# ScalarE's inputs of a state-space scan queued earlier, and two Toeplitz tables filled while it runs

## The chip, the cores and the metric

The kernel runs on one core of a Trainium2 chip. The metric is the device time of one execution in microseconds. A core has TensorE (matrix products, with a queue for weight loads), VectorE, ScalarE and GpSimd, and SyncE, which only issues transfers. Each engine takes its instructions in the order in which the program issues them, and engines wait for one another through semaphores.

## The reference

Two encoder layers of 512 tokens and 1024 channels. The change touches the mixer of the first: a projection to three parts, a gated depthwise convolution of 31 taps with a layer norm (`ya`), a bidirectional diagonal complex scan over 32 groups of 16 channels with 64 states (`yb`), and an output product. Feed-forward, neighbourhood attention and a second feed-forward follow.

```python
z = h @ w_in                                  # 1024 -> 512 za, 512 zg, 512 u
a = za * sigmoid(zg)
a = conv1d_depthwise(a, conv_w, taps=31) + conv_b
ya = silu(layer_norm(a, ln_g, ln_b))
# scan, for each direction: x_t = A x_{t-1} + coef * (B u_t); y_t = Re(C x_t)
dt = exp(log_step); mag = exp(lr * dt)
ar = mag * cos(li * dt); ai = mag * sin(li * dt)
y = y_fwd + y_bwd + d_skip * u
y = gelu(y)
yb = y * sigmoid(y @ glu_w + glu_b)
h = concatenate([ya, yb]) @ w_out
```

## The kernel before

All tokens stay on the chip. Weights stream from memory in chunks of 512 KB; `Weights` (lines 50 to 114) holds three raw buffers. The first 12 chunks (`ab_w_in`) are used as they land. Every later one is split by `split()` into `whi`, a rounded copy by ScalarE (line 89), and `wlo`, the rest by VectorE (line 91); then the next load is issued on SyncE's queue. `ahead()` splits two chunks beyond the current one, or, while `hold` is set, only loads.

The schedule is written by hand: what the program issues first on an engine runs first on it. Only VectorE's filling work is metered: `bgV.tick(ns)` adds a credit and issues steps of waiting generators as long as it is positive, and `charge` takes credit away. A step of 512 columns costs 75 + 512/0.96 = 608.

Stages in order, with the lines of the profile:

- Parameters and `u`: x is transposed and `u = xg @ W` is formed in four chunks (line 638). Between them VectorE makes the powers, phases and the first tables `PB` (`make_pb`). ScalarE writes `CT`, evicts `u` into `un` (line 677); `to_chunks` transposes that into `U`.
- The scan runs in eight pieces of four groups. `piece_t(i)` transposes `PB[i]` to `ppb` (evicted by ScalarE, 799) and copies two halves of C into `CB[i % 2]` (803); `piece_k(i)` multiplies `PB` by `CB` to kernel taps `kf` (813, 816); `piece_v(i)` multiplies `ppb` by `U` to `vt` (827, 830). `g_turn(i)` makes a phase table on VectorE, whose negated copy is ScalarE's (763). `g_scan(i)` is VectorE's work: ScalarE writes the decays `dk` in tile `rstdB` (770), then come a product with the phase, the scan instruction (781), a second product and sums into `S2`.
- In iteration i the order is `piece_v(i)`, three projection steps, T and K of piece i+2, four projection steps, `g_scan(i)`, `g_turn(i+2)`, `make_pb(i+4)`. A projection step (`heavy`, 694) is a matmul of zg or za, 64 in all; the last eight follow the loop, with VectorE's products `an` (703).
- Behind it `kd` is written to memory. The convolution (952) is a product of `AC`, the transposed `an`, with Toeplitz tables: 16 pieces n, two to a slot, three slots. `make_tc` fills a slot by 16 ScalarE instructions (925), each with a column of `mask16` as its factor; the first slot is filled by VectorE (930). Beside it VectorE makes the output tables `Q` (48 metered steps) and gathers each four pieces (960, 962).
- T (the banded kernel) is loaded from `kd` in three transfers (967, 969) issued behind the convolution. `out_y` needs T, `U`, `S2` and `Q`; the first is followed by the layer norm's mean (1026), its variance (1039), transposes (1052), the gelu, and the products `wo` and `glu`, which take split weights.

The lines around the change's largest move:

```python
piece_v(i); heavy(HV[0])
if i + 2 < NPC: pieces_tk(i + 2)      # P, ppb, CB, K, kf
heavy(HV[1]); run(g_scan(i))          # begins with ScalarE's decays
if i + 2 < NPC: run(g_turn(i + 2))    # ends with ScalarE's sign copy
if i + 4 < NPC: make_pb(i + 4)
```

Of the kernel before, what the change touches and what calls it, by code (L numbers as in the profile page):

```python
# [9 lines left out]
F32 = mybir.dt.float32  # L10
F32R = mybir.dt.float32r
I32 = mybir.dt.int32
AF = mybir.ActivationFunctionType
# [12 lines left out]
KW, VW = 64, 64  # L26
# [88 lines left out]
def tile_hybrid_encoder(ctx, tc, x, mix_norm, ffn_norm, ffn_w_gate, ffn_w_up, ffn_w_down,  # L115
# [60 lines left out]
    def psb(name="psb"):  # L176
        return psp.tile([P, 512], F32, tag="b", name=name, bufs=4)
# [154 lines left out]
    def pt(shape, name, pool=None, dt=F32):  # L332
        return (pool or mp).tile(shape, dt, tag=name, name=name)
# [19 lines left out]

    vecs = pt([NROW, P], "vecs", ep)
    work = pt([P, 2, 512], "work", ep)
    un = pt([P, G, 4, 16], "un", ep)
    lam = pt([96, 2, 64], "lam", ep)
    lst = pt([96, 2], "lst", ep)
    cwn = ep.tile([TAPS, 4, P], F32, tag="vt", name="cwn", bufs=2)
# [258 lines left out]
    for k in range(KD):  # L618
# [2 lines left out]
        A.activation(out=t, in_=pxs[k], func=AF.Copy)  # L621
        xT.append(t)


    pu = [psa("u") for _ in range(4)]
    for i in range(4):
# [7 lines left out]
        for kk in range(2):  # L634
            k = 2 * i + kk
            for j in range(4):
                c = slice(j * P, (j + 1) * P)
                PE.matmul(out=pu[j], lhsT=xg[:, k, c], rhs=w[:, kk], start=(k == 0), stop=(k == 7))
        if i == 1:
            rs0 = rsqrt(ss, 4, 1e-6, 1.0 / D)  # L640
            hrs = tmp([P, 4], "hrs", 1)
            V.tensor_scalar(out=hrs, in0=rs0, scalar1=0.5, scalar2=None, op0=ALU.mult)
# [22 lines left out]
        if i == 2:  # L665
            for r in range(2):
                ps = psb("ct")
                for t in range(4):
                    PE.transpose(out=ps[:, t * P:(t + 1) * P],
                                 in_=cnat[r][:, t].rearrange("p d n -> p (d n)"), identity=ident)  # L670
                A.activation(out=CT[:, r], in_=ps.rearrange("p (g c) -> p g c", c=16), func=AF.Copy,
                             scale=-1.0 if r else 1.0)
            for v, q, r, sg in ((0, 0, 0, 1.0), (0, 1, 1, 1.0), (1, 0, 1, -1.0), (1, 1, 0, 1.0)):
                A.activation(out=low[v][:, :, :, q], in_=et[:, r, :, 0].rearrange("p e g -> p g e"), func=AF.Copy,
                             scale=sg)
    for j in range(4):
        A.activation(out=un[:, :, j], in_=pu[j].rearrange("p (g c) -> p g c", c=16),
                     func=AF.Copy, scale=rs0[:, j:j + 1])


    an = pt([P, G, 4, 16], "an")
# [26 lines left out]
    def g_proj():  # L708
        yield from proj(True)
        yield from proj(False)  # L710

    proj_all = g_proj()

    def heavy(n):
        for _ in range(n):
# [33 lines left out]
    def g_turn(i):  # L749

        e = phases[i % 2]
        phase[i] = e
        sh = [P, 4, 8, 16]
        gs = slice(4 * i, 4 * i + 4)
        w = [pbt(sh) for _ in range(2)]
        for r in range(2):
            high = et[:, r, :, 1, gs].rearrange("p e g -> p g e").unsqueeze(3).to_broadcast(sh)
            lo = low[r][:, gs].rearrange("p g b q -> p g (b q)").unsqueeze(2).to_broadcast(sh)
            yield tt(w[r], high, lo, ALU.mult)
        yield tt(e[:, 1:3].rearrange("p q (n b) -> p n b q", b=8),  # L760
                 w[0].rearrange("p g a (b q) -> p (g a) b q", q=2),
                 w[1].rearrange("p g a (b q) -> p (g a) b q", q=2), ALU.add)
        A.activation(out=e[:, 0], in_=e[:, 2], func=AF.Copy, scale=-1.0)

    def g_scan(i):

        gs = slice(4 * i, 4 * i + 4)
        e = phase.pop(i)
        v, dk = vin.pop(i), decays[:, i % 2]
        A.activation(out=dk[:, :, 1:], in_=m8[:, 1, gs].unsqueeze(2).to_broadcast([P, 4, NCH - 1]), func=AF.Copy)  # L770
        m = work.rearrange("p o (q n) -> p o q n", q=2)
        z = tmp([P, 2, 256], "sqacc")

# [12 lines left out]
        yield tt(S2[0:64, :, gs, 1:NCH], mv[0:64, :, 0], mv[0:64, :, 1], ALU.add)  # L786
        yield tt(S2[64:128, :, gs, NCH - 2::-1], mv[64:128, :, 0], mv[64:128, :, 1], ALU.add)

    kd = dr.tile([8, 16, 1024], F32, name="kd")
    kf = pt([P, 2, G, 16], "kf", ep)  # L790
    ppb = xp.tile([P, 4, 2, 4, P], F32, tag="xgl", name="ppb")

    def piece_t(i):
        for q in range(2):
            ps = psb("P")
            for g in range(4):
                PE.transpose(out=ps[:, g * P:(g + 1) * P],
                             in_=PB[i][:, q, g].rearrange("p b c -> p (b c)"), identity=ident)
            A.activation(out=ppb[:, i % 4, q], in_=ps.rearrange("p (g n) -> p g n", g=4), func=AF.Copy)
        cb = CB[i % 2]  # L800
        for d in range(2):
            h = slice(64 * d, 64 * d + 64)
            A.activation(out=cb[h, :, :, d], in_=CT[h, :, 4 * i:4 * i + 4], func=AF.Copy)

    def piece_k(i):
        g0 = 4 * i
        pb, cb = PB.pop(i), CB[i % 2]
        pk = psb("K")
        for g in range(4):
            for q in range(2):  # L810
                w = pb[:, q, g].rearrange("p b c -> p (b c)")
                for c in range(0, P, KW):
                    PE.matmul(out=pk[c:c + KW, g * 32:g * 32 + 32], lhsT=w[:, c:c + KW],
                              rhs=cb[:, q, g].rearrange("p d c -> p (d c)"),
                              start=(q == 0), stop=(q == 1))
        A.activation(out=kf[:, :, g0:g0 + 4],
                     in_=pk[:, 0:128].rearrange("p (g d c) -> p d g c", g=4, d=2), func=AF.Copy)

    def piece_v(i):

        g0 = 4 * i
        pp = ppb[:, i % 4]
        pv = psb("v")
        for q in range(2):
            for g in range(4):
                for c in range(0, P, VW):
                    PE.matmul(out=pv[c:c + VW, (q * 4 + g) * 64:(q * 4 + g + 1) * 64], lhsT=pp[:, q, g, c:c + VW],
                              rhs=U[:, g0 + g] if c == 0 else U[:, g0 + g, ::-1], start=True, stop=True)
        v = ep.tile([P, 2, 256], F32, tag="vt", name="vt", bufs=2)
        A.activation(out=v, in_=pv.rearrange("p (q n) -> p q n", q=2), func=AF.Copy)  # L830
        vin[i] = v

    def pieces_tk(*ii):
        for i in ii:
            piece_t(i)
            piece_k(i)

    pieces_tk(0, 1)
    to_chunks(un, U)
    run(g_turn(0))  # L840
    make_pb(3)
    run(g_turn(1))
    for i in range(NPC):
        piece_v(i)
        heavy(HV[0])
        if i + 2 < NPC:
            pieces_tk(i + 2)
        heavy(HV[1])
        run(g_scan(i))
        if i + 2 < NPC:  # L850
            run(g_turn(i + 2))
        if i + 4 < NPC:
            make_pb(i + 4)
        if i == 1:
            V.tensor_tensor(out=gqk, in0=col[:, R_QK:R_QK + 1], in1=col[:, R_QK + 1:R_QK + 2], op=ALU.mult)
    for h in range(2):
        PL.tensor_tensor(out=pair[:, 64 * h:64 * h + 64], in0=ident[:, 0:64], in1=ident[:, 64:128], op=ALU.add)
    PL.tensor_scalar(out=pair, in0=pair, scalar1=1.0 / 512, scalar2=1.0, op0=ALU.mult, op1=ALU.mult)
# [20 lines left out]
    nc.sync.dma_start(out=kd_ap(9, 3), in_=kfr[16:64, 1])  # L879
    PL.dma_start(out=kd_ap(7, 1), in_=kfr[0:16, 1], accum_op=ALU.add)  # L880

    V.tensor_reduce(out=mask16, in_=ident.rearrange("p (b c) -> p c b", c=16), axis=AX.X, op=ALU.add)
    heavy(100)
    W.hold = False
    early.close()
# [21 lines left out]
    for h in range(2):  # L907
        src = conv_b[0, 256 * h:256 * h + 256]
        nc.sync.dma_start(out=cbB[64 * h:64 * h + 64],
                          in_=bass.AP(tensor=src.tensor, offset=src.offset, ap=[[0, 64], [1, 256]]))  # L910
    tca = lp.tile([P, 2, 2, 2, 16, NLAG], F32, name="tca", tag="tca")
    slots = [tca[:, 0], tca[:, 1]]
    wvs = wv.rearrange("p (h s) l -> p h s l", h=2)
    tcs = {}

    def make_tc(n, cnt=2):

        t = slots[n // 2 % 3]
        for i in range(cnt):
            tcs[n + i] = t[:, :, (n + i) % 2]  # L920
        t = t[:, :, n % 2:n % 2 + cnt]
        w = wvs[:, :, n:n + cnt]
        if n > 1:
            for c in range(16):
                A.activation(out=t[:, :, :, c], in_=w, func=AF.Copy, scale=mask16[:, c:c + 1])
            return
        sh = [P, 16, NLAG]
        for h in range(2):
            for i in range(cnt):
                V.tensor_tensor(out=t[:, h, i], in0=w[:, h, i].unsqueeze(1).to_broadcast(sh),  # L930
                                in1=mask16.unsqueeze(2).to_broadcast(sh), op=ALU.mult)
        bgV.charge(1700 * cnt)

    job_q = {(i, hf): g_q(i, hf) for i, hf in ((0, 0), (2, 0), (0, 1), (2, 1), (1, 0), (3, 0), (1, 1), (3, 1))}
    bgV.fill += job_q.values()
    make_tc(0, 1)
    make_tc(1, 1)
    slots.append(xp.tile([P, 2, 2, 16, NLAG], F32, tag="xgh", name="tcb"))
    tick(1000)
    to_chunks(an, AC[:, :, 2:NCH + 2])  # L940
    make_tc(2)
    make_tc(4)
    yc = pt([P, LCH, 16, 16], "an")
    lns = tmp([P, 4, LCH], "lns", 1)
    for b in range(4):
        ps = psa("conv")
        for gi in range(4):
# [8 lines left out]
            if n % 2 and n + 5 < 16:  # L956
                make_tc(n + 5)
            tick(2200)
        gs = slice(4 * b, 4 * b + 4)
        V.tensor_tensor(out=yc[:, :, gs], in0=ps.rearrange("p (g c t) -> p t g c", g=4, t=LCH),  # L960
                        in1=cbB[:, gs].unsqueeze(1).to_broadcast([P, LCH, 4, 16]), op=ALU.add)
# [548 lines left out]
```

## Time and profile before

| | us |
|---|---|
| median of 3 runs | 1277.01 (1276.51 to 1278.05) |
| profiled execution | 1276.18 |
| its span | 1274.5 |
| TensorE busy | 1218.3 (96%) |
| VectorE busy | 676.6 (53%) |
| ScalarE busy | 466.6 (37%) |

The span is what the profiler covers; the execution is a little longer. Busy time is an average over stages: a matmul's end is modelled, and an engine that waits for another counts as idle. In what follows, a wait is put down to the instruction that came last, and the timeline's start times count from the start of the span.

### The profile page before, as it was taken

Reading aid. Unit: us, or ns where it says so; the run is one execution under the profiler, and the core shown is the slowest. Engines: PE = TensorE matmul, PEld = TensorE weight load, DVE = VectorE, ACT = ScalarE, POOL = GpSimd, SP = SyncE. Lnnn points to the kernel's source line nnn. Section 1 sums busy time; section 2 is a strip of 40 time slices with the busy share of each in tenths; the row PEclk is TensorE's granted clock in tenths of the full one; section 3 lists DMA queues with packets and bytes.
Section 4 is the critical chain, followed back from the end, with each engine's and each line's share of the span. In section 5 each row is a group of like instructions: output and inputs, shape, how many; then the busy total and the mean of one; then the engine's idle time right before and its main releaser. Section 6 shows DMA issues by size and latency. Waiting matters only on the chain.

```text
span 1274.5 us, 16175 instructions
## 1 busy us (share of the span) xinstructions
PE 1218.3 (96%) x6427; PEld 962.4 (76%) x6427; DVE 676.6 (53%) x1165; ACT 466.6 (37%) x823; POOL 36.7 (3%) x90
## 2 busy tenths in 40 slices
PE   7887967899999999999999999999999999999998
PEld 4544467688888888888888887667888888888886
DVE  7897896665444444333335753655544444443322
ACT  4523296543323322222225455553432233222110
POOL 1000000000000000000000001430000000000000
PEclk9988999899999999999999999999999999999999
DMA  7411230333333333333344353212233333332321
GB/s 154 89 34 34 68 86 2 100 99 88 95 99 97 93 93 99 94 102 93 91 136 157 116 165 104 72 51 66 84 104 95 99 99 100 99 99 86 128 100 33
DMA packets 173154, 118.04 MB, mean 93 GB/s; under 512 B 21193, under 2 KB 153593, under 8 KB 173080
## 3 DMA queue, kind: packets, MB, share of 16 engines
q1 hardware_dynamic: 172616, 115.92, 31.4%
q10 hardware_dynamic: 400, 1.07, 0.4%
q8 instruction: 50, 0.82, 0.3%
q14 instruction: 24, 0.20, 0.0%
q0 software_dynamic: 64, 0.03, 0.0%
HBM read 109.04 MB, written 7.96 MB: 92 GB/s over the span
## 4 chain that ended last, share of the span: by engine, by line
PE 89%; ACT 5%; DVE 3%; DMA 1%; SPq 1%; issue 1%; POOL 0%; DVEq 0%; ACTq 0%; POOLq 0%
PE up L199 6%; PE gate L199 6%; PE gate L200 6%; PE up L200 6%; PE gate L201 6%; PE up L201 6%; PE qkv L1375 3%; PE qkv L1377 3%; PE qkv L1376 3%; PE dn L199 3%; PE dn L201 3%; PE dn L200 3%; PE dn L1476 3%; PE dn L1474 3%; PE dn L1475 3%; PE o L1337 3%
## 5 line engine op out<-in xcount | busy, mean ns | idle before, releaser
L91 DVE TENSOR_TENSOR wlo<-wraw,whi 128x1024 fp32r<-128x1024 f32 x176 | 212.9, 1213 | 262.6 <-ACT whi L89 261.3
L89 ACT ACTIVATE whi<-wraw 128x1024 fp32r<-128x1024 f32 x176 | 183.5, 1045 | 288.9 <-issue 113.9
L199 PE MATMUL gate<-xgh,whi 128*128 128x512 f32 x352 | 137.2, 390 | 0.0
L199 PE MATMUL up<-xgh,whi 128*128 128x512 f32 x352 | 137.1, 390 | 0.0
L201 PE MATMUL gate<-xgh,wlo 128*128 128x512 f32 x352 | 137.0, 389 | 0.0
L201 PE MATMUL up<-xgh,wlo 128*128 128x512 f32 x352 | 137.0, 389 | 0.0
L200 PE MATMUL gate<-xgl,whi 128*128 128x512 f32 x352 | 136.9, 389 | 0.0
L200 PE MATMUL up<-xgl,whi 128*128 128x512 f32 x352 | 136.9, 389 | 0.0
L1159 DVE TENSOR_TENSOR fu<-up,rstdB 128x512 f32<-128x512 f32 x44 | 30.4, 691 | 113.3 <-PE up L201 113.3
L1161 ACT ACTIVATE gh<-fu 128x512 fp32r<-128x512 f32 x44 | 27.8, 632 | 150.8 <-DVE fu L1160 150.8
L201 PEld LDWEIGHTS gate<-xgh,wlo 128*128 128x128 f32 x352 | 66.1, 188 | 14.0
L199 PEld LDWEIGHTS gate<-xgh,whi 128*128 128x128 f32 x352 | 66.1, 188 | 13.7
L201 PEld LDWEIGHTS up<-xgh,wlo 128*128 128x128 f32 x352 | 66.1, 188 | 13.8
L199 PEld LDWEIGHTS up<-xgh,whi 128*128 128x128 f32 x352 | 66.0, 188 | 13.8
L200 PEld LDWEIGHTS up<-xgl,whi 128*128 128x128 f32 x352 | 66.2, 188 | 13.6
L200 PEld LDWEIGHTS gate<-xgl,whi 128*128 128x128 f32 x352 | 66.0, 187 | 13.4
L199 PE MATMUL dn<-gh,whi 128*128 128x512 f32 x176 | 69.3, 394 | 0.0
L200 PE MATMUL dn<-gl,whi 128*128 128x512 f32 x176 | 69.3, 394 | 0.0
L201 PE MATMUL dn<-gh,wlo 128*128 128x512 f32 x176 | 69.3, 394 | 0.0
L1476 PE MATMUL dn<-whi,gl 128*128 128x512 f32 x176 | 69.2, 393 | 0.0
L1474 PE MATMUL dn<-whi,gh 128*128 128x512 f32 x176 | 69.0, 392 | 0.0
L1375 PE MATMUL qkv<-whi,xgh 128*128 128x512 f32 x176 | 68.8, 391 | 0.0
(293 smaller groups left out, 2053.6 us busy)
## 6 DMA issues: line engine op xcount, KB each, us to landing
wraw<-in_ffn_w_gate_dram SPq DMA_DIRECT2D x44, 512.0 KB
wraw<-in_ffn_w_up_dram SPq DMA_DIRECT2D x44, 512.0 KB
wraw<-in_ffn_w_down_dram SPq DMA_DIRECT2D x38, 512.0 KB
wraw<-in_na_w_qkv_dram SPq DMA_DIRECT2D x24, 512.0 KB
wraw<-in_ab_w_in_dram SPq DMA_DIRECT2D x12, 512.0 KB
bt<-bd SPq DMA_DIRECT2D x8, 640.0 KB
wraw<-in_ab_w_out_dram SPq DMA_DIRECT2D x8, 512.0 KB
wraw<-in_na_w_out_dram SPq DMA_DIRECT2D x8, 512.0 KB
```

What stands on the lines that cost most here:

```text
L89: self.nc.scalar.activation(out=hi, in_=raw, func=AF.Copy)
L91: eng.tensor_tensor(out=lo, in0=raw, in1=hi.bitcast(F32), op=ALU.subtract)
L199: PE.matmul(out=o, lhsT=lh, rhs=rh, start=start, stop=False)
L200: PE.matmul(out=o, lhsT=lh, rhs=rl, start=False, stop=False)
L201: PE.matmul(out=o, lhsT=ll, rhs=rh, start=False, stop=stop)
L1337: PE.matmul(out=o[64 * e:64 * e + 64, j * P:(j + 1) * P], lhsT=vt[p0:p0 + n, kt, hc:hc + 64], rhs=pt_[p0:p0 + n, b, e], start=(b == 0), st ...
L1375: PE.matmul(out=pq[j], lhsT=lh, rhs=wh[:, kk], start=(k == 0), stop=False)
L1376: PE.matmul(out=pq[j], lhsT=lh, rhs=wl[:, kk], start=False, stop=False)
L1377: PE.matmul(out=pq[j], lhsT=ll, rhs=wh[:, kk], start=False, stop=(k == 7))
L1474: PE.matmul(out=pd[j], lhsT=gh[:, k, c], rhs=wh[:, kk], start=(k == 0), stop=False)
L1475: PE.matmul(out=pd[j], lhsT=gh[:, k, c], rhs=wl[:, kk], start=False, stop=False)
L1476: PE.matmul(out=pd[j], lhsT=gl[:, k, c], rhs=wh[:, kk], start=False, stop=(k == NF - 1))
```

## The change

`un` moves into the tile that also holds `ppb`, which has two slots instead of four. Of the four evictions of `u`, two go to VectorE. `piece_t` no longer copies C; `make_cb` does, two pieces ahead, and piece 0's P and K are issued between chunks of `u`. The sign copy and the decays become `scan_tables(i)`, issued an iteration ahead of their scan. The two-slot tile `tca` is allocated beside the scan's buffers, `mask16` is formed in iteration 1, and from iteration 2 on six table instructions follow each iteration (`tc_early`, slots for n = 0 to 3); VectorE's fill goes. In the convolution, `W.ahead()` is called behind the second group.

```diff
-    un = pt([P, G, 4, 16], "un", ep)
+    half_xgl = xp.tile([P, 2, 2048], F32, tag="xgl", name="un_ppb")
+    un = half_xgl[:, 0].rearrange("p (g j c) -> p g j c", g=G, j=4)
+    ppb = half_xgl[:, 1].rearrange("p (s q g n) -> p s q g n", s=2, q=2, g=4)
...
+    def make_cb(i):
+        cb = CB[i % 2]
+        for d in range(2):
+            h = slice(64 * d, 64 * d + 64)
+            A.activation(out=cb[h, :, :, d], in_=CT[h, :, 4 * i:4 * i + 4], func=AF.Copy)
...
+            if k == 6:
+                piece_k(0)
...
+            make_cb(0)
+            make_cb(1)
+            piece_t(0)
...
     for j in range(4):
-        A.activation(out=un[:, :, j], in_=pu[j].rearrange("p (g c) -> p g c", c=16),
-                     func=AF.Copy, scale=rs0[:, j:j + 1])
+        v = pu[j].rearrange("p (g c) -> p g c", c=16)
+        if j % 2:
+            V.tensor_scalar(out=un[:, :, j], in0=v, scalar1=rs0[:, j:j + 1], scalar2=None, op0=ALU.mult)
+        else:
+            A.activation(out=un[:, :, j], in_=v, func=AF.Copy, scale=rs0[:, j:j + 1])
...
+    tca = pt([P, 2, 2, 2, 16, NLAG], "tca")
+    def g_tc(n):
+        t = slots[n // 2 % 3]
+        for i in range(2):
+            tcs[n + i] = t[:, :, i]
+        for c in range(16):
+            A.activation(out=t[:, :, :, c], in_=wvs[:, :, n:n + 2], func=AF.Copy, scale=mask16[:, c:c + 1])
+            yield 1
+    def g_tc_early():
+        yield from g_tc(0)
+        yield from g_tc(2)
...
+    def scan_tables(i):
+        e = phase[i]
         A.activation(out=e[:, 0], in_=e[:, 2], func=AF.Copy, scale=-1.0)
+        A.activation(out=decays[:, i % 2, :, 1:], in_=m8[:, 1, 4 * i:4 * i + 4].unsqueeze(2).to_broadcast([P, 4, NCH - 1]),
+                     func=AF.Copy)
...
-        A.activation(out=dk[:, :, 1:], in_=m8[:, 1, gs].unsqueeze(2).to_broadcast([P, 4, NCH - 1]), func=AF.Copy)
...
-    pieces_tk(0, 1)
+    piece_t(1)
     to_chunks(un, U)
+    piece_k(1)
+    make_cb(2)
+    make_cb(3)
     run(g_turn(0))
     make_pb(3)
     run(g_turn(1))
+    scan_tables(0)
+    tc_early = g_tc_early()
     for i in range(NPC):
         piece_v(i)
         heavy(HV[0])
         if i + 2 < NPC:
-            pieces_tk(i + 2)
+            piece_t(i + 2)
+            piece_k(i + 2)
+        if i + 4 < NPC:
+            make_cb(i + 4)
         heavy(HV[1])
+        if i + 1 < NPC:
+            scan_tables(i + 1)
         run(g_scan(i))
...
         if i == 1:
+            V.tensor_reduce(out=mask16, in_=ident.rearrange("p (b c) -> p c b", c=16), axis=AX.X, op=ALU.add)
+        if i > 1:
+            for _ in range(6):
+                next(tc_early, 0)
...
-    V.tensor_reduce(out=mask16, in_=ident.rearrange("p (b c) -> p c b", c=16), axis=AX.X, op=ALU.add)
...
-    make_tc(0, 1)
-    make_tc(1, 1)
+    for _ in tc_early:
+        pass
...
     to_chunks(an, AC[:, :, 2:NCH + 2])
-    make_tc(2)
     make_tc(4)
...
             if n % 2 and n + 5 < 16:
                 make_tc(n + 5)
             tick(2200)
+        if b == 1:
+            W.ahead()
         gs = slice(4 * b, 4 * b + 4)
```

## Rows read from the trace of the kernel before

**Rows 1.** The page: busy tenths of 40 slices; costliest groups (busy, mean ns | idle).
```profile
PE   7887967899999999999999999999999999999998
...
L91 DVE TENSOR_TENSOR wlo<-wraw,whi 128x1024 fp32r<-128x1024 f32 x176 | 212.9, 1213 | 262.6 <-ACT whi L89 261.3
```

**Rows 2.** Waits, 20 to 240 us: who waited <- for whom: total us, times, longest.
```profile
ACT phase L763 <- DVE phase L436: 42.5, 6, 8.4
...
DVE sqacc L781 <- ACT rstdB L770: 12.1, 4, 4.1
...
DVE work L436 <- ACT vt L830: 3.9, 3, 1.9
```

**Rows 3.** Timeline of VectorE (start, duration us, instruction, [idle <-releaser]), the scan's ends.
```profile
48.02 0.69 DVE L436 TENSOR_TENSOR pb<-work 128x512 f32<-128x512 f32 x1
...
59.70 1.22 DVE L436 TENSOR_TENSOR work<-phase,vt 128x1024 f32<-128x1024 f32 x1 [1.94 <-ACT vt L830]
...
153.75 0.37 DVE L882 TENSOR_REDUCE mask<-ident 128x16 f32<-128x128 f32 x1
```

**Rows 4.** Timeline of TensorE, end of u, one iteration, the projection's last records.
```profile
38.91 7.03 PE L638 MATMUL u<-wraw,xg 128*128 128x512 f32 x16
...
52.89 3.79 PE L729 MATMUL U<-ident,un 64*64 64x64 f32 x64
...
67.39 1.15 PE L827 MATMUL v<-U,ppb 128*64 128x64 f32 x32
...
71.15 1.04 PE L797 MATMUL P<-ident,pb 128*128 128x128 f32 x8
...
73.56 1.12 PE L813 MATMUL K<-CB,pb 128*64 128x32 f32 x32 [1.37 <-ACT CB L803]
...
144.64 13.14 PE L694 MATMUL za<-wraw,xg 128*128 128x512 f32 x30
```

**Rows 5.** Timeline of TensorE from the convolution to the gate product.
```profile
158.57 3.93 PE L729 MATMUL U<-ident,an 64*64 64x64 f32 x64 [0.78 <-DVE an L703]
...
195.08 3.44 PE L952 MATMUL conv<-tca,AC 128*64 128x128 f32 x40 [1.66 <-ACT tca L925]
...
203.03 0.32 PE L985 MATMUL y<-T,U 128*64 128x128 f32 x1
...
206.17 1.06 PE L1026 MATMUL mean<-lns,wpad 128*128 128x8 f32 x8
...
218.39 1.39 PE L1052 MATMUL yT<-ident,yn 64*128 64x64 f32 x29
...
227.65 0.80 PE L199 MATMUL wo<-mah,whi 128*128 128x512 f32 x1 [7.87 <-ACT whi L89]
...
241.22 0.39 PE L199 MATMUL glu<-ygs,whi 128*128 128x512 f32 x1
```

**Rows 6.** Timeline of ScalarE, convolution and weight split.
```profile
159.36 4.91 ACT L732 ACTIVATE AC<-U 64x512 f32<-64x512 f32 x8 [11.99 <-DVE tca L930]
...
164.30 5.21 ACT L925 ACTIVATE tca<-wv,mask 128x160 f32<-128x160 f32 x16
...
226.56 2.94 ACT L89 ACTIVATE whi<-wraw 128x1024 fp32r<-128x1024 f32 x3
```

**Rows 7.** Groups by shape of VectorE, 150 to 210 us (busy us, mean ns | idle).
```profile
L436 DVE TENSOR_TENSOR sq<-pwQ,CT 128x512 f32<-128x512 f32 x32 | 20.8, 687 | 0.5
...
L703 DVE TENSOR_TENSOR an<-an,za 128x512 f32<-128x512 f32 x4 | 2.7, 684 | 1.8 <-PE za L694 1.8
```

**Rows 8.** Timeline of SyncE's queue (issue time and length).
```profile
159.66 0.61 SPq L967 DMA_DIRECT2D T<-kd  x1
```

**Rows 9.** Windows: us, busy us of each engine, granted clock, DMA share, GB/s.
```profile
164.00:166.00 2.00, 1.87 (x25) 1.62 (x21) 1.93 (x4) 1.97 (x7) 0.00 (x0) 1.00 0.99 205
...
172.00:173.00 1.00, 1.00 (x13) 0.77 (x9) 0.00 (x0) 1.00 (x5) 0.00 (x0) 1.00 0.06 16
...
231.00:234.00 3.00, 3.00 (x11) 2.35 (x11) 2.81 (x6) 2.08 (x4) 0.00 (x0) 0.73 1.00 333
```

More of the change, by code (lines that the diff above doesn't have):

```diff
@@ L622, in tile_hybrid_encoder, with piece_t, piece_k @@
         xT.append(t)
+    kd = dr.tile([8, 16, 1024], F32, name="kd")
+    kf = pt([P, 2, G, 16], "kf", ep)
+    def piece_t(i):
+        for q in range(2):
+            ps = psb("P")
+            for g in range(4):
+                PE.transpose(out=ps[:, g * P:(g + 1) * P],
+                             in_=PB[i][:, q, g].rearrange("p b c -> p (b c)"), identity=ident)
+            A.activation(out=ppb[:, i % 2, q], in_=ps.rearrange("p (g n) -> p g n", g=4), func=AF.Copy)
+    def make_cb(i):
[3 more added lines that the diff above has]
+            A.activation(out=cb[h, :, :, d], in_=CT[h, :, 4 * i:4 * i + 4], func=AF.Copy)
+    def piece_k(i):
+        g0 = 4 * i
+        pb, cb = PB.pop(i), CB[i % 2]
+        pk = psb("K")
+        for g in range(4):
+            for q in range(2):
+                w = pb[:, q, g].rearrange("p b c -> p (b c)")
+                for c in range(0, P, KW):
+                    PE.matmul(out=pk[c:c + KW, g * 32:g * 32 + 32], lhsT=w[:, c:c + KW],
+                              rhs=cb[:, q, g].rearrange("p d c -> p (d c)"),
+                              start=(q == 0), stop=(q == 1))
+        A.activation(out=kf[:, :, g0:g0 + 4],
+                     in_=pk[:, 0:128].rearrange("p (g d c) -> p d g c", g=4, d=2), func=AF.Copy)
     pu = [psa("u") for _ in range(4)]
@@ L712, in tile_hybrid_encoder, with make_tc @@
     proj_all = g_proj()
+    tca = pt([P, 2, 2, 2, 16, NLAG], "tca")
+    slots = [tca[:, 0], tca[:, 1]]
+    wvs = wv.rearrange("p (h s) l -> p h s l", h=2)
+    tcs = {}
+    def g_tc(n):
[5 more added lines that the diff above has]
+            yield 1
+    def make_tc(n):
+        for _ in g_tc(n):
+            pass
+    def g_tc_early():
+        yield from g_tc(0)
+        yield from g_tc(2)
     def heavy(n):
@@ L787, in g_scan @@
         yield tt(S2[64:128, :, gs, NCH - 2::-1], mv[64:128, :, 0], mv[64:128, :, 1], ALU.add)
[L789 to L817, printed above, removed]
     def piece_v(i):
         g0 = 4 * i
-        pp = ppb[:, i % 4]
+        pp = ppb[:, i % 2]
         pv = psb("v")
@@ L831, in piece_v @@
         vin[i] = v
[L833 to L836, printed above, removed]
-    pieces_tk(0, 1)
+    piece_t(1)
     to_chunks(un, U)
+    piece_k(1)
+    make_cb(2)
+    make_cb(3)
     run(g_turn(0))
@@ L910, in tile_hybrid_encoder @@
                           in_=bass.AP(tensor=src.tensor, offset=src.offset, ap=[[0, 64], [1, 256]]))
[L911 to L932, printed above, removed]
     job_q = {(i, hf): g_q(i, hf) for i, hf in ((0, 0), (2, 0), (0, 1), (2, 1), (1, 0), (3, 0), (1, 1), (3, 1))}
     bgV.fill += job_q.values()
-    make_tc(0, 1)
-    make_tc(1, 1)
+    for _ in tc_early:
+        pass
     slots.append(xp.tile([P, 2, 2, 16, NLAG], F32, tag="xgh", name="tcb"))
```

## Prediction

> **What bounds the kernel now.** I read the page first. TensorE is busy at 90% or more of every slice of 32 us from the ninth on, and below that only in the first eight [rows 1], so a change in the scan and the convolution can win time only before about 255 us; behind it the kernel is a run of matmuls that moves as one block. Then I read the waits of 20 to 240 us. VectorE's scan waits 12.1 us for `rstdB` (the decays, L770) and 3.9 us for `vt`; ScalarE stands 42.5 us behind VectorE's `phase` [rows 2]. These are one knot: the sign copy of `phase` (L763) is queued on ScalarE behind a turn that VectorE makes last in an iteration, and `vt`, `ppb`, CB, `kf` and the decays all stand behind it. VectorE then waits for the decays.
>
> VectorE sets the scan's length: its first scan instruction comes at 59.70, its last ends just before the mask sum at 153.75 [rows 3]. TensorE needs less. An iteration's v, P and K cost 1.15, 1.04 and 1.12 us, and a record of the projection 13.14 / 30 = 0.44 us [rows 4]; 8 v, 6 P, 6 K and 128 records give 9.2 + 6.2 + 6.7 + 56.1 = 78 us.
>
> From 164.30 ScalarE sets the convolution: it fills seven slots, 5.1 us each (16 instructions, 5.21 us), and TensorE, whose share of a slot is 3.4 us, waits for each [rows 5, 6]. The transposes end at 219.8 and `wo` begins at 227.65, after a wait of 7.87 for `whi` [rows 5], because ScalarE splits the output weights only behind half of the gelu.
>
> **Scan.** All decays and sign copies are now queued one iteration before their use, CB two before, so the decay waits of 12.1 go. Of the `vt` waits 1.94 us is ahead of the first scan and 1.96 later; the later ones go too, since `vt` no longer stands behind the turn just made. VectorE's work from first to last scan is 94.0 - 12.1 - 2.0 = 79.9 us.
>
> Its start hardly moves. VectorE ends its third pb at 48.7, two evictions of `un` are new there, and two turns and a pb then take it, unbroken before, to 57.76 (59.70 less 1.94) [rows 3]. A PSUM eviction by VectorE of 128x512 with a column factor has no row. The nearest, `an` times `za` from PSUM, takes 0.68 [rows 7]; I take that, 1.4 for both, and keep 0.4 to 1.0 each. So it is free at 59.1. TensorE gets there: u ends at 45.94 [rows 4] plus P and K of piece 0, about 48; `un` is complete at 50.1 and the U transposes start there, 2.7 before 52.89 [rows 4]; `vt` was ready at 59.67, and 2.7 less plus about 1.5 for kf and the four CB copies queued ahead is 58.5. The scan starts at 59.1, 0.6 earlier.
>
> VectorE ends at 59.1 + 79.9 + 0.4 (the mask sum, moved into the loop) = 139.4, and the four products of `an` make it 142.1. TensorE: from v at 55.2 plus 78 is 133, plus what its P wait for pb, which VectorE makes two iterations ahead. It has 6 us for that and stays hidden. The table fills, 32 instructions of 0.32 us, are ScalarE work in six iterations, 1.9 us each, in a queue that has just lost 42.5 us of waiting; `vt` of the next iteration is still 5 us or more ahead of VectorE, and without that cover each would cost VectorE up to 1.9. So the transposes of `an` start at 142.1, not 158.57: **16.5 us**, with 12 to 17.5 as ends (the low one lets TensorE come 4.5 us behind VectorE, by waits or a slower clock).
>
> **Convolution.** Taking the start at 142.1: evictions of AC end 5.7 later as now (164.27 against 158.57), at 147.8. Two slots are ready, so ScalarE fills six: slots 4, 6, 8, 10, 12 end at 152.9, 158.0, 163.1, 168.2, 173.3. Alone this saves one fill, 5.1. But `W.ahead()` at b = 1 comes behind slot 12: two `whi` (0.98 each, from three in 2.94 [rows 6]) take ScalarE to 175.3, slot 14 ends at 180.4 and the convolution at 183.9. That is 19.1 before the 203.0 of now.
>
> What is queued behind the added wait matters more. **VectorE:** eight ticks of 2200 plus those of 1000 and 2000 and a credit of 560, less 1200, at 608 each emit 33 of the 48 Q steps ahead of `wlo`. At 0.69 each [rows 7] plus the first output group (two more of that length) it reaches `wlo` at 166.2 and stands until `whi` lands at 174.3, 8 us. Then two `wlo` (1.21 each [rows 1]), the second group, 15 Q steps (10.3) and the third take it to about 189.8, and `lns` of the last group is there at 191.2. **SP:** each split issues a weight load that waits for `wlo`, and the three transfers of T are queued behind both. T was issued at 159.66 [rows 8]; now it is 176.9. T took 12.3 us to its last bytes at about 172 [rows 9]; one load more ahead of it (0.5 MB at 222 GB/s, 2.4) makes 191.6. The first y needs T. So y starts near 191.3 instead of 203.03, the TensorE having stood since 183.9, and of 19.1 us 7.4 are given back.
>
> Such a gap drops the clock: after the idle stretch of 7.87 us a record of `wo` takes 0.80 us where glu's takes 0.39, and the granted clock of 231 to 234 is 0.73, a mean of half and full 2.4 GHz [rows 5, 9]. The first y group and its mean (3.1 us now) then need 1.5 to 2.5 more; I take 2.0, and so the mean starts at 196.5, **9.7 us** before 206.17. From there to the transposes the chain of mean, square, var and scale is ScalarE and VectorE and moves as it is.
>
> For T's speed the trace has two rows, 205 GB/s while T loads and 333 GB/s while weights load [rows 9]. The Trainium skill (DMA: Bandwidth & Descriptors, Specifications) gives about 358 GB/s as the HBM limit of a core; by it, as an estimate, T would be there near 187. This trace disagrees for T, 205 GB/s. I go by T's own row; what the other row's rate would do is rival C.
>
> **Weights at `wo`.** Slots 12 and 13 are split by then, so `wo` no longer waits for `whi`: 7.87 us go [rows 5]. What is late next is TensorE itself, its transposes; `mal` is made in the order in which `wo` takes it. Its slow clock goes too: from 227.65 to the first glu are 13.57 us for 48 matmuls, and at the warm 0.23 they need 10.9, **2.6** more. Glu needs ygs; ScalarE has one `whi` instead of three between the gelus, 2 us less, and glu's third group would meet ygs within 0.5 us, so I cost it at 0 to 0.5.
>
> **Sum.** 9.7 + 7.9 + 2.6 = 20.2, less 0.2 for ygs: 20.0 off the profiled execution's 1276.18 us (span 1274.5 and 1.7 around it) is 1256.2. That execution lies 0.8 under the median 1277.01, so the median becomes 1257.0; because every later stage is a block, nothing is added there.
>
> **Rivals.** *A, as summed:* 0.58. Its own range, scan 12 to 17.5, clock 0 to 3, T 189 to 194: 1252 to 1263.
>
> *B, the scan gives half.* VectorE finds `vt` or the sign copy late again, because ScalarE is now blocked one turn earlier and carries the fills. For it: rows 2 show how long that queue stood. Against: the turn that it waits for is a whole iteration old. At 8 us of 16.5 the time is 1265.5, between 1261 and 1270. 0.16.
>
> *C, T and the clock cost little.* T arrives before VectorE is through: 3.15 MB (two loads and T) at 333 GB/s is 9.5 us after 176.9, then `lns` at 191.2 sets the mean, 15.0 before now, and 15.0 + 7.9 + 2.6 = 25.5 gives 1251.5; if VectorE also doesn't stand at `wlo` it is down to 1247. 0.18.
>
> *D, slower: T late.* The mechanism is the SP queue: T behind two loads that hang on `wlo`, itself behind five table fills. For it: T's issue falls 35 us behind the AC evictions' start instead of 1. Each us of T's landing is a us of the end, and only `wo` gains against it. From T at 191.6 and a gain of 20, it breaks even at 211.6 and is slower by over 0.2% from 214; it would take 37 us to land instead of 12.3. At 217 the time is 1282. No row shows T's bytes at such a rate. 0.03.
>
> *E, no change:* the edit's order is undone by waits that cover whole tiles (`un` and `ppb` now share one), and the scan keeps its old pace: 20.0 - 16.5 leaves 3.5, 1273.5, and with T at its late end, 194, the time is 1276. 0.05.
>
> **How the numbers follow.** The time is A's, 1257. A, C and most of B are 1248 to 1268; outside lie the edges of B and C, D and E. A measurement of this kernel can tell 0.2% (2.6 us) from no change. Faster 0.92 (A, B, C), same 0.05, slower 0.03.
>
> **What would show it.** VectorE's waits for `rstdB` gone and its last scan near 139; the `an` transposes near 142; ScalarE with six fills, two `whi` behind the fifth; VectorE standing about 8 us for `whi`; T issued near 177 and TensorE idle 5 to 8 us ahead of the first y, at half clock after it; `wo` without its wait. I am wrong if VectorE waits for ScalarE inside the scan, if T is issued before the fills, or if glu waits for ygs by more than 2 us.

## The result, and the profile after

| | before | after |
|---|---|---|
| median of 4 runs | 1276.84 us (1276.51 to 1278.05) | 1257.97 us (1256.29 to 1258.42) |
| ratio, 95% interval | | 0.9848 (0.9831 to 0.9865) |
| profiled execution, its span | 1276.18, 1274.5 us | 1258.42, 1256.5 us |
| the scan's last instruction ends | 153.8 us | 139.8 us |
| transposes of `an` start | 158.57 us | 142.36 us |
| T issued, first y | 159.66, 203.03 us | 178.48, 192.71 us |
| `mean`, `wo`, first glu | 206.17, 227.65, 241.22 us | 198.05, 211.59, 222.78 us |

The change takes 18.9 us off the median, and by the profile 18.4 of it is there at the first glu (241.22 to 222.78). From there the kernel moves as a block, as [rows 1] had it: the two spans differ by 18.0.

The waits of the kernel after, between 20 and 240 us (who waited <- for whom: total, times, longest):

```profile
ACT phase L828 <- DVE phase L438: 16.9, 3, 7.4
...
DVE wlo L91 <- ACT whi L89: 10.1, 5, 9.1
...
PE y L1008 <- DMA T<-kd: 6.9, 1, 6.9
```

ScalarE's wait at `phase` falls from 42.5 us [rows 2] to 16.9, and `rstdB` and `vt` are gone from VectorE's list. VectorE's wait at `wlo` has grown, from 2.0 us in all, and TensorE's at T is new. The timeline of VectorE (start, duration, instruction, idle time ahead and its releaser) shows both ends of the scan, and then the new wait:

```profile
49.02 1.40 DVE L716 TENSOR_SCALAR un_ppb<-u,rs_y 128x512 f32<-128x512 f32 x2
...
59.37 1.22 DVE L438 TENSOR_TENSOR work<-phase,vt 128x1024 f32<-128x1024 f32 x1
...
138.42 1.37 DVE L438 TENSOR_TENSOR S<-work 64x504 f32<-64x504 f32 x2
...
175.09 2.36 DVE L91 TENSOR_TENSOR wlo<-wraw,whi 128x1024 fp32r<-128x1024 f32 x2 [9.07 <-ACT whi L89]
```

The first line is the two evictions that came from ScalarE, 0.70 us each. The scan starts at 59.37, no instruction of VectorE waits in it, and the last S ends at 139.8. At 166.0 VectorE runs dry: it stands 9.07 us at `wlo`, with the last three output groups, their `lns` (the sums for the layer norm's mean) and the remaining Q steps queued behind it. ScalarE's timeline says why:

```profile
143.58 4.91 ACT L794 ACTIVATE AC<-U 64x512 f32<-64x512 f32 x8 [10.28 <-DVE sq L438]
...
168.92 5.19 ACT L765 ACTIVATE tca<-wv,mask 128x160 f32<-128x160 f32 x16
174.02 1.99 ACT L89 ACTIVATE whi<-wraw 128x1024 fp32r<-128x1024 f32 x2
175.91 5.19 ACT L765 ACTIVATE tca<-wv,mask 128x160 f32<-128x160 f32 x16
```

Two `whi` come between the fifth and the sixth fill. The idle 10.28 ahead of the evictions of AC, which the trace puts down to an `sq` of VectorE, is ScalarE standing until the `an` transposes come; before it was 11.99 [rows 6]. SyncE's queue (start and length of each issue):

```profile
176.35 0.37 SPq L72 DMA_DIRECT2D wraw<-in_ssm_glu_w_dram  x1
177.48 0.82 SPq L72 DMA_DIRECT2D wraw<-in_ab_w_out_dram  x1
178.48 0.61 SPq L990 DMA_DIRECT2D T<-kd  x1
```

T is issued behind the two weight loads, 18.8 us later than before [rows 8]. TensorE's timeline puts it together (xN counts the records of a line):

```profile
123.50 13.14 PE L734 MATMUL za<-wraw,xg 128*128 128x512 f32 x30
142.36 4.46 PE L791 MATMUL U<-ident,an 64*64 64x64 f32 x64 [5.72 <-DVE an L743]
...
174.17 3.44 PE L973 MATMUL conv<-tca,AC 128*64 128x128 f32 x40 [1.66 <-ACT tca L765]
181.16 4.70 PE L973 MATMUL conv<-tca,AC 128*64 128x128 f32 x40 [3.55 <-ACT tca L765]
192.71 0.66 PE L1008 MATMUL y<-T,U 128*64 128x128 f32 x2 [6.86 <-DMA T<-kd]
...
198.05 1.06 PE L1049 MATMUL mean<-lns,wpad 128*128 128x8 f32 x8
...
211.59 0.50 PE L199 MATMUL wo<-mah,whi 128*128 128x512 f32 x1
...
222.78 0.39 PE L199 MATMUL glu<-ygs,whi 128*128 128x512 f32 x1
```

The conv block at 174.17 is the usual one. The next waits 3.55 us, because the `whi` sit ahead of its fill, and takes 4.70 us instead of 3.44. The first y then waits 6.86 us for T, its group and the mean come slowly, and `wo` follows the transposes with no wait, where [rows 5] had 7.87 us. Windows of the kernel after (us, busy us and count of TensorE, its weight loads, VectorE, ScalarE, GpSimd, granted clock, DMA share, GB/s) show the clock in each of these places:

```profile
142.00:144.00 2.00, 1.64 (x28) 1.64 (x29) 1.91 (x4) 0.42 (x1) 0.00 (x0) 0.50 0.00 0
182.00:184.00 2.00, 2.00 (x18) 2.00 (x17) 1.93 (x4) 0.00 (x0) 0.00 (x0) 0.53 1.01 221
188.00:190.00 2.00, 0.00 (x0) 0.00 (x0) 1.93 (x4) 0.00 (x0) 0.00 (x0) 1.00 1.07 213
193.00:196.00 3.00, 3.00 (x30) 3.00 (x29) 0.00 (x0) 0.00 (x0) 0.00 (x0) 0.50 0.00 0
```

A granted clock of 0.50 is 1.2 GHz, the lower level: during the `an` transposes, behind a wait of 5.72 us; for most of the conv block behind the 3.55 (0.53); and after the wait for T. From the first y to the mean are 5.34 us, where [rows 5] had 3.14.

### The profile page after: what moved, and what is told of

Read it like the earlier page. It is cut to its first block, busy times and chain, and to the rows that moved or that the text cites. A ratio compares the mean times of both kernels' runs of the same rounds, so it can differ in the third digit from the quotient of the medians.

```text
span 1256.5 us, 16175 instructions
## 1 busy us (share of the span) xinstructions
PE 1213.6 (97%) x6427; PEld 961.7 (77%) x6427; DVE 674.1 (54%) x1163; ACT 470.1 (37%) x837; POOL 37.1 (3%) x90
## 4 chain that ended last, share of the span: by engine, by line
PE 84%; ACT 3%; DMA 1%; DVE 1%; issue 0%; SPq 0%; POOL 0%; ACTq 0%; DVEq 0%; POOLq 0%
PE up L199 6%; PE gate L199 6%; PE gate L201 6%; PE up L201 6%; PE gate L200 6%; PE up L200 6%; PE qkv L1398 3%; PE qkv L1400 3%; PE qkv L1399 3%; PE dn L200 3%; PE dn L199 3%; PE dn L201 3%; PE dn L1499 3%; PE dn L1497 3%; PE dn L1498 3%; PE o L1360 3%
## 5 line engine op out<-in xcount | busy, mean ns | idle before, releaser
L201 PEld LDWEIGHTS gate<-xgh,wlo 128*128 128x128 f32 x352 | 66.0, 188 | 13.9
L200 PEld LDWEIGHTS gate<-xgl,whi 128*128 128x128 f32 x352 | 66.1, 188 | 13.6
L199 PEld LDWEIGHTS up<-xgh,whi 128*128 128x128 f32 x352 | 66.0, 188 | 13.6
```

The costliest lines, as they stand in the source:

```text
L199: PE.matmul(out=o, lhsT=lh, rhs=rh, start=start, stop=False)
L200: PE.matmul(out=o, lhsT=lh, rhs=rl, start=False, stop=False)
L201: PE.matmul(out=o, lhsT=ll, rhs=rh, start=False, stop=stop)
```

## Experiments

Four kernels ran on one chip (before: 1277.06 us there, 7 runs), the later four on another (1276.97, 7 runs). Each time is the median of four runs, its range in brackets; the ratio, with its 95% interval, is to before. Theory: the scan's 16 us come from the tables and the copies of C, and the early weight split takes back at T and at `wlo` what it gives at `wo`. Rivals: the split is worth its 7.9 us; the fills or the evictions are the gain. In the profiles of e1, e2 and e3, whose code is that of the change up to the convolution, the transposes of `an` start at 141.27 to 141.56, in after at 142.36: about 1 us of what these profiles gain over after does not come from their edits.

**e1: the change without the early split.**

```diff
-        if b == 1:
-            W.ahead()
```

> The changed kernel without the early split of two weight chunks in the convolution. Theory (what the early split wins at wo it gives back through T and VectorE): ScalarE ends its sixth table at 179.1 instead of 181.1, TensorE keeps its full clock, the convolution ends at 182.5, T is issued near 138 and has landed long before, VectorE does not stand for whi, the mean starts at 185.8 instead of 198.05 (12.3 earlier). In exchange wo waits about 7.9 us for whi again and runs its first records at half clock (2.6 us). Net 1.8 us faster than the changed kernel: 1256. Rival (the early split is where the gain of the change came from): about 10 us slower than the changed kernel, 1268.

1254.31 us (1254.18 to 1255.69), ratio 0.9820 (0.9804 to 0.9836): 3.7 us faster than the whole change. The two intervals touch, but the slowest run of e1 is below the fastest of after (1256.29). TensorE's timeline, the mean and the first record of `wo`:

```profile
184.47 1.06 PE L1047 MATMUL mean<-lns,wpad 128*128 128x8 f32 x8
...
205.95 0.79 PE L199 MATMUL wo<-mah,whi 128*128 128x512 f32 x1 [7.87 <-ACT whi L89]
```

T is issued at 137.78, the mean comes 13.6 us earlier than in after, and `wo` waits its old 7.87 us and runs slowly behind it (13.21 us from `wo` to glu, against 11.19). 13.6 - 7.9 - 2.0 = 3.7. So the split that removes a wait of 7.9 costs more than it removes. The theory had the sign right and gave the split a smaller loss, about 2; without the 0.8 us that e1's profile is ahead at the transposes of `an` the loss is nearer 3 than 4.

**e2: T's tile and its three transfers ahead of the convolution's loop, all else as in the change.**

```diff
     make_tc(4)
+    T = xp.tile([P, LCH, G, 16], F32, tag="xgl", name="T")
+    nc.sync.dma_start(out=T[0:64]..., in_=kd_ap(0, 4, 4, 1024))
...
-    T = xp.tile([P, LCH, G, 16], F32, tag="xgl", name="T")
```

> The changed kernel with the three transfers of T issued ahead of the convolution's loop, so ahead of the two weight loads on the queue; the early split stays where it is. Theory: T lands before 155; TensorE still ends the convolution at 185.9 and VectorE still stands 9 us for whi, so the first y group starts at once, and the mean waits for VectorE's last group of lns at 191.4 instead of starting at 198.05: 6.6 us earlier, 1251.4. Rival (memory traffic, not the place in the queue, sets T's landing): no change, 1258. Rival (VectorE's standing costs nothing): mean at 189, 1249.

1251.55 us (1250.63 to 1251.94), ratio 0.9795 (0.9780 to 0.9811): 6.4 us less than after, from where three DMAs stand in SyncE's queue. T is issued at 139.07 and y follows the convolution at once. SyncE's queue, then TensorE's timeline:

```profile
139.07 0.61 SPq L966 DMA_DIRECT2D T<-kd  x1
...
180.08 3.12 PE L979 MATMUL conv<-tca,AC 128*64 128x128 f32 x37 [3.56 <-ACT tca L765]
...
186.07 0.83 PE L1049 MATMUL mean<-lns,wpad 128*128 128x8 f32 x6
190.40 0.59 PE L1049 MATMUL mean<-lns,wpad 128*128 128x8 f32 x2 [3.49 <-DVE lns L991]
```

and VectorE's:

```profile
174.01 2.36 DVE L91 TENSOR_TENSOR wlo<-wraw,whi 128x1024 fp32r<-128x1024 f32 x2 [9.08 <-ACT whi L89]
...
189.66 0.69 DVE L991 TENSOR_REDUCE lns<-an 128x8 f32<-128x512 f32 x1
```

VectorE still stands 9.08 us for `whi`, so the last `lns` ends at 190.35 and the mean's last two records wait for it, 3.49 us. The Trainium skill (DMA: Bandwidth & Descriptors, Anatomy of one DMA — SWDGE (gpsimd) path) says, in a section on transfers that GpSimd issues, that a semaphore wait happens on the issuing sequencer before dispatch. For SyncE's queue the traces agree: T, which itself waits for nothing there, was issued at 178.48 behind two loads that wait for `wlo`, and at 139.07 ahead of them.

**e3: the split behind T's transfers, at the convolution's end.**

```diff
-        if b == 1:
-            W.ahead()
...
     for o in range(2):
         nc.sync.dma_start(out=T2[64:128, :, o], in_=kd_ap(1 + o, 4, 4))
+    W.ahead()
```

> The changed kernel with the early split moved behind the convolution's loop and behind T's transfers, so that neither T nor VectorE's filling work stands behind it. Theory: the convolution ends at 182.5, T is there, the mean starts at 185.8, both splits are done by about 187 on engines that wait for the mean, wo follows its transposes without a wait: 12.3 us faster than the changed kernel, 1245.7. Rival (the early place of the split is needed to hide it): VectorE's two wlo (2.4 us) push the mean's subtraction and the gain is 8 us or less, 1250.

1244.64 us (1243.52 to 1245.84), ratio 0.9742 (0.9726 to 0.9759): 13.3 us less than after, 9.7 less than no early split at all. TensorE:

```profile
177.88 3.12 PE L973 MATMUL conv<-tca,AC 128*64 128x128 f32 x37 [1.66 <-ACT tca L765]
...
183.88 1.06 PE L1048 MATMUL mean<-lns,wpad 128*128 128x8 f32 x8
...
197.42 0.50 PE L199 MATMUL wo<-mah,whi 128*128 128x512 f32 x1
```

and VectorE:

```profile
182.09 0.69 DVE L983 TENSOR_REDUCE lns<-an 128x8 f32<-128x512 f32 x1
182.69 2.35 DVE L91 TENSOR_TENSOR wlo<-wraw,whi 128x1024 fp32r<-128x1024 f32 x2
184.97 2.35 DVE L1052 TENSOR_TENSOR an<-an,mean 128x1024 f32<-128x1024 f32 x2
```

The conv block waits 1.66 us, not 3.55, and takes no longer than the others; the mean comes at 183.88; `wlo` is made behind the last `lns` with no wait; `wo` doesn't wait either. ScalarE has nothing else to do between its last fill and the mean, so the two `whi` at 177.74 cost nothing there.

**e4: the change without `scan_tables`; sign copy and decays where they were before.**

```diff
+        A.activation(out=e[:, 0], in_=e[:, 2], func=AF.Copy, scale=-1.0)
...
+        A.activation(out=dk[:, :, 1:], in_=m8[:, 1, gs]..., func=AF.Copy)
...
-        if i + 1 < NPC:
-            scan_tables(i + 1)
```

> The changed kernel with the sign copy of phase and the decays issued where they were before (behind the turn that makes the phase, and at the head of the scan); CB two pieces ahead, the early fills and the split stay. Theory (the place of these two copies in ScalarE's order is what held VectorE): VectorE waits for rstdB and vt inside the scan again, 8 to 16 us in all, the transposes of an start that much later than 142.4, and the time is 1266 to 1274. Rival (CB two pieces ahead, which frees TensorE's K, is what won the scan): no more than 2 us slower, 1260.

1268.36 us (1267.35 to 1271.84), ratio 0.9932 (0.9907 to 0.9958): as forecast, 10.4 us of the change's 18.9 go. Its waits, 50 to 165 us:

```profile
ACT phase L825 <- DVE phase L438: 47.7, 7, 9.8
...
DVE work L438 <- ACT vt L869: 6.7, 3, 2.9
...
DVE sqacc L849 <- ACT rstdB L838: 5.5, 3, 2.8
```

The knot is back: 47.7 us of ScalarE behind VectorE, and VectorE's two waits behind that; `an` is transposed 11.2 us later, at 153.60.

**e8: the tables alone, in the kernel before.**

```diff
...
+    scan_tables(0)
     for i in range(NPC):
...
+        if i + 1 < NPC:
+            scan_tables(i + 1)
         run(g_scan(i))
```

> The kernel before with one part of the change alone: sign copy and decays issued one iteration ahead (scan_tables). Theory (these two copies are what held the scan): VectorE's waits for rstdB go, the transposes of an start at 143 to 145 instead of 158.57, everything behind keeps its length, 1262 to 1264. Rival (the parts need each other, as ScalarE still holds CB behind ppb): half of that, 1270.

1263.03 us (1260.67 to 1264.38), ratio 0.9894 (0.9877 to 0.9910): 13.9 us from moving two small copies. The profiled execution was the fastest of the four, 2.4 us below the median, so that its times show a little more than that. TensorE, and VectorE's last product of `an`:

```profile
94.17 1.12 PE L817 MATMUL K<-CB,pb 128*64 128x32 f32 x32 [1.25 <-ACT CB L807]
...
142.72 3.92 PE L729 MATMUL U<-ident,an 64*64 64x64 f32 x64 [0.78 <-DVE an L703]
...
190.33 1.06 PE L1033 MATMUL mean<-lns,wpad 128*128 128x8 f32 x8
...
141.98 0.69 DVE L703 TENSOR_TENSOR an<-an,za 128x512 f32<-128x512 f32 x1 [0.71 <-PE za L694]
```

The transposes start at 142.72, as early as with the whole change; K still waits about 1.25 us for CB in each of six iterations, 7.6 us in all. That costs little here, but it leaves nothing to spare: VectorE's last product of `an` waits 0.71 us for the projection.

**e7: e3 with the copies of C back beside their own piece.**

```diff
...
             piece_t(i + 2)
+            make_cb(i + 2)
             piece_k(i + 2)
-        if i + 4 < NPC:
-            make_cb(i + 4)
```

> The kernel with the late split (e3_split_late, 1244.6) and in it the copies of C made with their own piece, behind ppb, as before. Theory (TensorE has about 5.7 us to spare at the end of the scan, VectorE sets its length): K waits 0.6 to 1.3 us for CB in each of six iterations, TensorE uses up its slack and the transposes of an start 0 to 2 us later: 1244.6 to 1246.5. Rival (CB two pieces ahead is a main part of the scan's gain): 5 us or more slower, 1250.

1248.06 us (1245.67 to 1249.23), ratio 0.9771 (0.9756 to 0.9785): 3.4 us slower than e3, between what the two theories gave. The two intervals touch, so that it is slower is likely, and its size is not shown. TensorE:

```profile
56.02 1.95 PE L863 MATMUL v<-U,un_ppb 128*64 128x64 f32 x32
...
95.32 1.12 PE L650 MATMUL K<-CB,pb 128*64 128x32 f32 x32 [1.31 <-ACT CB L640]
...
107.61 1.12 PE L650 MATMUL K<-CB,pb 128*64 128x32 f32 x32 [2.80 <-ACT CB L640]
...
147.01 3.93 PE L790 MATMUL U<-ident,an 64*64 64x64 f32 x64 [0.78 <-DVE an L742]
```

VectorE, and the projection's last records in e3:

```profile
146.27 0.69 DVE L742 TENSOR_TENSOR an<-an,za 128x512 f32<-128x512 f32 x1 [1.03 <-PE za L733]
...
125.68 13.14 PE L734 MATMUL za<-wraw,xg 128*128 128x512 f32 x30
```

K waits 1.3 us in four iterations, 2.80 in one and 1.24 in the last: 9.3 us in all, and TensorE had nothing to spare for that: in e3 the projection ends at 138.82, where VectorE's first product of `an` starts at 138.85. The projection now ends last: VectorE waits for `za` at each product of `an`, and the transposes start at 147.01, 5.6 us later than in e3. The profiled execution was the slowest of the four (1249.23, 5.7 over that of e3); by the medians it is 3.4. The copies' place does not explain it alone: e8 has them in the same place, and its projection ends 4.3 us earlier. K waits 1.7 us less there, and the rest is TensorE's clock: in e7 it ran at 0.50 to 0.53 around the first v (1.95 us instead of 1.15) and at 0.52 to 0.62 behind the wait of 2.80. Copying C two pieces ahead was not run alone on the kernel before.

**e6: e3 with the first two slots filled after the scan, as before.**

```diff
-        if i > 1:
-            for _ in range(6):
-                next(tc_early, 0)
...
+            V.tensor_tensor(out=slots[0][:, h, i], in0=wvs[:, h, i]..., in1=mask16..., op=ALU.mult)
...
     to_chunks(an, AC[:, :, 2:NCH + 2])
+    make_tc(2)
     make_tc(4)
```

> The kernel with the late split (e3_split_late, 1244.6) and in it the fills of the first two table slots behind the scan, as they were before: the first by VectorE, the second by ScalarE behind the evictions of AC. Theory (fills during the scan cost nothing there and save one of seven fills in the convolution): the convolution ends 5.1 us later, 1249.7, and the scan ends where it did. Rival (the early fills delay vt or the sign copies by some of their 10.3 us, so taking them out shortens the scan): 1246 or less.

1249.62 us (1249.04 to 1252.50), ratio 0.9790 (0.9775 to 0.9804): 5.0 us slower than e3. TensorE:

```profile
141.14 4.33 PE L791 MATMUL U<-ident,an 64*64 64x64 f32 x64 [4.00 <-DVE an L743]
...
152.55 5.78 PE L976 MATMUL conv<-tca,AC 128*64 128x128 f32 x37 [3.70 <-ACT tca L765]
...
189.16 1.06 PE L1051 MATMUL mean<-lns,wpad 128*128 128x8 f32 x8
```

The transposes start at 141.14, 0.25 us earlier than e3's 141.39: nearly all of the 10.3 us of fill instructions lies hidden in the scan. The second conv slot waits 3.70 us for the fill that is back in the queue, and the mean comes 5.3 us later than e3's 183.88. One fill is 5.1 us.

**e5: e3 with all four evictions of `u` on ScalarE again.**

```diff
-        if j % 2:
-            V.tensor_scalar(out=un[:, :, j], in0=v, scalar1=rs0[:, j:j + 1], ...)
-        else:
-            A.activation(out=un[:, :, j], in_=v, func=AF.Copy, scale=rs0[:, j:j + 1])
+        A.activation(out=un[:, :, j], in_=v, func=AF.Copy, scale=rs0[:, j:j + 1])
```

> The kernel with the late split (e3_split_late, 1244.6) and in it all four evictions of un on ScalarE again. Theory (VectorE sets the scan's length from its first turn on, so work put on it ahead of the scan is paid in full): VectorE is free for its first turn 1.4 us earlier, the scan and the transposes of an come 1.0 to 1.4 earlier, 1243.4. Rival (VectorE's evictions bring U, and by that vt, earlier): the first scan waits for vt and the time is the same or up to 1 us longer.

1243.15 us (1242.86 to 1243.48), ratio 0.9735 (0.9720 to 0.9749), the lowest median here. VectorE takes 9.16 us from the end of its third pb to the first scan instruction, where e3 took 10.26; 1.1 us of the expected 1.4 is there. The intervals to before overlap, so that e5 beats e3 is likely and not shown; that it beats before (33.8 us) and after (14.8 us) is.

From before down to e5 the differences are: tables 13.9, early fills 5.0, copies of C 3.4, a split at the right place 9.7, evictions left on ScalarE 1.5 (not shown); 33.5 of 33.8 us. They are not steps of one chain: the tables were measured alone, the fills and the copies by taking them out of e3, and taken out of the change the tables are worth 10.4 (e4). That the sum comes out is partly luck.

## Why the prediction was right, point by point

**Scan, 16.5 us forecast, 16.2 measured.** Every step came: start 59.37 (59.1), no wait inside, end 139.8 (139.4), transposes at 142.36 (142.1). The `un` evictions cost 0.70 each, the price of the nearest row in [rows 7]. The cause is the tables, by e4 and e8. The cover that the fills needed held (e6), and so did TensorE's, but it was thinner than the 6 us of the prediction: the projection ends at 136.64, 3.2 us ahead of VectorE's first product of `an`, and P's two waits for pb, which the sum left open, took 2.7 of it. In e3's profile it was nothing, as TensorE ran at 0.50 behind the same two waits.

**Convolution, the mean 9.7 us earlier forecast, 8.1 measured.** This is the one term mis-sized by more than 0.5, by 1.6 us, and T's issue accounts for it: 178.48, not 176.9. 0.7 was there when ScalarE reached `whi` (174.02, not 173.3). The `an` transposes started 0.3 later, and they ran at half clock and took 4.46 us instead of 3.93, which put the end of the evictions of AC, in the sum "as now", 0.4 later. The rest is in SyncE's queue: T goes 1.00 us behind the second load, which itself takes 0.82; the sum had let T go 0.2 behind `wlo`. The mechanism was as forecast: VectorE standing 9.07 us (8), the wait for T, 6.86 us, and half clock behind it, 2.2 us (2.0). Not forecast was the half clock in the last conv block; it makes the block 1.3 us longer, and T hides that. Two slips in the working changed next to nothing: y was put at 191.3 although T, which it needs, was put at 191.6, and the last of the forty slices in [rows 1] is an 8, so TensorE is below 90% there too.

**Weights at `wo`.** The wait of 7.87 is gone, and from `wo` to glu are 11.19 us instead of 13.57: 2.4 us of clock (2.6). Glu does not wait for `ygs`. So 8.1 + 7.9 + 2.4 = 18.4 us, where the sum had 20.0.

**Rivals.** B needed VectorE to wait for ScalarE inside the scan; it doesn't. C failed at its premise, that T loads at 333 GB/s and is there before VectorE is through: in 186 to 190 us it moved at 213 to 223, and y waited for it until 192.71. What C said would follow from an early T is borne out where T is early: 1251.55 in e2 (C's 1251.5), and 6.9 less in e3, where VectorE doesn't stand either. D's queue does cost something, 6.4 us (e2), but T was there 14.2 us behind its issue, far under the 37 us that D needed to make the kernel slower. E fell with the scan.

What the prediction saw and did not draw out: the sum had T's delay on one side and `wo` on the other, and called their difference a gain; beside a kernel without the early split it is a loss of 3.7 us (e1).

## What to carry to other kernels

When an instruction is moved earlier to remove a wait, list for each engine and each DMA queue what then stands behind it: here a split moved to save 7.9 us held up VectorE for 9.1 us and T's transfers by about 40, and the same split a dozen lines further down saved the 7.9 and held up nothing. Before a large rearrangement, look for the smallest instruction in the longest wait: two copies of 0.4 us, queued one iteration earlier, were worth 13.9 us alone, and without them the change kept 8.5 of its 18.9. Cover shrinks as the bound engine gets faster. In the kernel before, K waited 16.6 us for the copies of C and VectorE still ended the scan last:

```profile
PE K L813 <- ACT CB L803: 16.6, 6, 7.4
```

With the tables moved, 7.6 us of such waits left TensorE level with VectorE (e8), and with 9.3 us it ended last (e7).

## What the hardware showed that was not expected

A wait of 3.55 us behind several of 1.66 was followed in after by a granted clock of 0.53 and a conv block of 4.70 us, and one of 3.70 in e6 by 0.50; blocks behind 1.66 alone ran at full clock in 3.44. But the length of the wait doesn't decide it: in e2 a block behind 3.56 us ran at 1.00, as long as e3's behind 1.66, and so did the second block of the kernel before, behind 3.70:

```profile
169.57 3.44 PE L952 MATMUL conv<-tca,AC 128*64 128x128 f32 x40 [3.70 <-ACT tca L925]
```

The transposes of `an`, which had run at full clock behind a wait of 0.78 us (3.93 us [rows 5]), ran at 0.50 behind the wait of 5.72 and took only 4.46: half the clock costs 0.5 us where ScalarE's evictions, 0.61 us each, set the pace, and 2.2 us in y, where nothing else does. What decides between the two levels was not tried. T moved at 213 to 223 GB/s in after (186 to 190 us), where TensorE and ScalarE stood, and at 205 to 221 before (164 to 170 us), where ScalarE and VectorE were both busy: its rate hardly differed between the two stages. What sets it was not tried either.
